# The four merge products of a hybrid encoder block: from channel form to token form

## The chip, the cores and the metric

The kernel runs on one core of a Trainium2 chip. The metric is the device time of one execution in microseconds (us), lower is better. The core has TensorE (PE, matmuls, with a separate row PEld for its weight loads), VectorE (DVE), ScalarE (ACT) and GpSimd (POOL), and queues that start DMAs; the weights come through the queue of SyncE (SP). Each engine works through its own list of instructions in order.

## What is computed

A block with 256 tokens and 2048 channels: a gated linear attention (GLA) branch and a Hyena branch run side by side, are merged by two sigmoid gates, projected, and followed by LayerNorm and an MLP. The part that the change touches is the merge:

```python
y_gla = _gla_branch(q, k, v, r, af, ab, ...)
y_hy = _hyena_branch(hy_u, ...)
g = jax.nn.sigmoid(gate_logits).reshape(B, L, N_BRANCH, D)
merged = g[:, :, 0, :] * (y_gla @ w_gla_o) + g[:, :, 1, :] * (y_hy @ w_hy_o)
mix = merged @ w_out
h = _layernorm(DEEPNORM_ALPHA * h + mix, ln1_g, ln1_b)
```

The gate logits are two more products of the input x, with 2048 columns each. So four products of size 256 x 2048 x 2048 make up the merge. The kernel calls them g1 (first gate), go (GLA output), g2 (second gate) and ho (Hyena output).

## The kernel before

**Products.** Every fp32 operand is split into a high and a low part (`split_hi_lo`, L80): ScalarE casts the high part (L81), VectorE subtracts it from the source for the low part (L82). A product is then high x high + high x low + low x high. Weights come in blocks of 128 x 2048 values, 1 MB each (L95), and each block is split in two halves of 1024 columns (`whi`, `wlo`, three buffers each).

There are two forms of a product:

- **Channel form** (`channel_pair`, L157, with `channel_products`, L136): the result has channels on partitions and tokens along the row. The weights are loaded into TensorE, and the activations move through: for each of 16 slices of the 2048 inputs, one matmul with the high weights moves 512 columns (256 tokens, high and low part side by side, L142), and one with the low weights moves 256 (L146). A block of weights gives 128 channels. ScalarE copies the low half of the PSUM bank out (L154), and VectorE adds the high half to it (L155): `channel_sum`, at high priority.
- **Token form** (`token_group`, L198, with `token_products`, L183): the result has tokens on partitions and 512 channels along the row. The activations are loaded into TensorE, and 512 columns of weights move through: for each slice and each of the two halves of the tokens, three matmuls (L194 to L196). Four blocks of weights give 512 channels, in two PSUM banks, and nothing has to be added afterwards.

Before the change, the products r and v of GLA, the projection w_out (wo) and the second MLP product (w2) are in token form; the rest are in channel form, the four merge products among them.

**Order of the work.** All blocks of weights lie in the order of use in one array `wblk`. Side work (GLA heads, Hyena chunks, filters) is put off by `later(d, fn)` (L110), which runs a function `d` blocks later, when `pump` (L114) is called after a block; `drain` (L122) runs all that is left. A scheduler at build time then sets the order of each engine's list by the order in the program, priorities and its own estimate of when operands are ready; `tc.high_priority()` puts instructions ahead.

**Around the merge.** During the v products and g1 (L632) the side work is GLA's heads: gates (`gla_gates`, L480, with the exponentials and logarithms L504, L505, L517), scores and outputs (`gla_out`, L585). Its last step is a chain over ScalarE (L212, L213) and VectorE (L214 to L217, L599) that ends in the transposes yt on TensorE (L606). The g1 results lie in the buffers `q_sb` and `k_sb`; their sigmoids (L638) stand in the program behind all of this. Then come 8 Hyena chunks of 6 blocks each (uv, ux, uz), with the go products spread among them by `go_after` (L750), in pairs of blocks; each pair is multiplied into the g1 gates (L748). Then g2 with its sigmoids (L773), a drain, and ho, whose results are multiplied by the second gate (L785), added (L786) and split (L787) into `mT`, which has channels on partitions, as w_out needs it. `mT` shares its buffer with the input `xT`. The w_out products follow (L864). Matmuls write to PSUM banks: four for the products (`mmp`), four for the side work (`sdp`).

Of the kernel before, what the change touches and what calls it, by code (L numbers as in the profile page):

```python
# [9 lines left out]
F32 = mybir.dt.float32  # L10
F32R = mybir.dt.float32r
I32 = mybir.dt.int32
AF = mybir.ActivationFunctionType
ALU = mybir.AluOpType
DRAM = bass.MemoryType.DRAM

P = 128
# [23 lines left out]
def block_kernel(  # L41
# [38 lines left out]
    def split_hi_lo(hi, lo, src):  # L80
        nc.scalar.copy(hi, src)  # L81
        nc.vector.tensor_tensor(lo, src, hi.bitcast(F32), op=ALU.subtract)  # L82
# [74 lines left out]
    def channel_pair(act, name, dst=None, scale=1.0):  # L157
        if dst is None:
            dst = base.tile([P, 2, L], F32, tag="sum", name=f"{name}_s")
        for c in range(2):  # L160
            ps = channel_psum(f"{name}_{c}")
            parts = next_block()
            for h in range(2):
                channel_products(ps, act, parts[h], range(8 * h, 8 * h + 8))
            channel_sum(dst[:, c], ps, f"{name}_l{c}", scale)
            pump()
        return dst
# [458 lines left out]

    m_sb = [q_sb, k_sb]

    def m_pair(c2):
        return m_sb[c2 // 4][:, 2 * (c2 % 4):2 * (c2 % 4) + 2, :]  # L630

    for c2 in range(8):  # L632
        channel_pair(xT, f"g1_{c2}", m_pair(c2))
    drain()
    gstk.close()
    for c2 in range(8):
        mp = m_pair(c2)
        nc.scalar.activation(mp, mp, AF.Sigmoid)  # L638


    hstk = ExitStack()
# [98 lines left out]

    go_done = [0]

    def gla_o_pair():
        c2 = go_done[0]
        go_done[0] += 1
        ps = channel_pair(yT, f"go{c2}")
        mp = m_pair(c2)
        nc.vector.tensor_tensor(mp, mp, ps, op=ALU.mult)  # L748

    go_after = [0, 0, 1, 1, 1, 1, 1, 3]  # L750
    for c in range(NCH):
        ps = channel_pair(xT, f"uv{c}")
        cst[("v", c)] = short_conv(ps, 2 * c, f"cv{c}", "cv", 2)
        later(1, hy_v(c))
        later(3, hy_fwd(c, 0))
        later(3, hy_mul(c, 0))
        ps = channel_pair(xT, f"ux{c}")
        cst[("x1c", c)] = short_conv(ps, 16 + 2 * c, f"cx{c}", "cx", 1)
        later(1, hy_x1(c))
        later(5, hy_inv(c, 0))  # L760
        later(6, hy_fwd(c, 1))
        later(6, hy_mul(c, 1))
        ps = channel_pair(xT, f"uz{c}")
        cst[("x2", c)] = short_conv(ps, 32 + 2 * c, f"cz{c}", "cz", 2)
        later(8, hy_inv(c, 1))
        for _ in range(go_after[c]):
            gla_o_pair()


    g2_sb = qp.tile([P, KT, L], F32, tag="G", name="g2_sb")  # L770
    for c2 in range(8):
        ps = channel_pair(xT, f"g2_{c2}")
        nc.scalar.activation(g2_sb[:, 2 * c2:2 * c2 + 2, :], ps, AF.Sigmoid)  # L773
    drain()
    yhT = act_tile(base, "yT", "yh")
    for c in range(NCH):
# [1 line left out]
        nc.gpsimd.dma_start(yr, yh_dram[c])  # L778
        split_hi_lo(yhT[:, 2 * c:2 * c + 2, 0], yhT[:, 2 * c:2 * c + 2, 1], yr)
    mT = act_tile(base, "xT", "mT")  # L780
    for c2 in range(8):
        ps = channel_pair(yhT, f"ho{c2}")
        gp2 = g2_sb[:, 2 * c2:2 * c2 + 2, :]
        mp = m_pair(c2)
        nc.vector.tensor_tensor(gp2, gp2, ps, op=ALU.mult)  # L785
        nc.vector.tensor_tensor(mp, mp, gp2, op=ALU.add)  # L786
        split_hi_lo(mT[:, 2 * c2:2 * c2 + 2, 0], mT[:, 2 * c2:2 * c2 + 2, 1], mp)  # L787
    hstk.close()
    qkg.close()

# [184 lines left out]
def _layout(a):  # L975
    import numpy as np

    f = np.float32

    def chan(w):  # L980
        k, n = w.shape
        return w.reshape(k // P, P, n // P, P).transpose(2, 1, 0, 3).reshape(n // P, P, -1)

    def tok(w):
        k, n = w.shape
        return (w.reshape(k // 512, 4, P, n // 512, 512).transpose(3, 0, 2, 1, 4)
                .reshape(-1, P, D))

    w_in = a["w_in"][0]
    names = ["q", "k", "v", "r", "af", "ab", "u", "g"]  # L990
    sizes = [1024, 1024, 2048, 2048, 16, 16, 6144, 4096]
    seg, s = {}, 0
    for n, z in zip(names, sizes):
        seg[n] = w_in[:, s:s + z]
        s += z
    z16 = np.zeros((D, 32), f)
    ga = np.concatenate([seg["af"], seg["ab"]] * 3 + [z16], axis=1)
    u = chan(seg["u"]).reshape(3, NCH, 2, P, D)
    go = chan(a["w_gla_o"][0])
    ubl, gi = [], 0  # L1000
    for c, n in enumerate([0, 0, 1, 1, 1, 1, 1, 3]):
        for t in range(3):
            ubl.append(u[t, c])
        ubl.append(go[gi:gi + 2 * n])
        gi += 2 * n
    f1 = chan(a["w_ff1"][0])
    w2 = a["w_ff2"][0]
    f1q = [f1[16 * i:16 * (i + 1)] for i in range(QT)]
    f2q = [tok(w2[D * i:D * (i + 1)]) for i in range(QT)]
    g1, g2 = chan(seg["g"][:, :D]), chan(seg["g"][:, D:])  # L1010
    wblk = np.concatenate(
        [chan(ga), chan(seg["q"]), chan(seg["k"]), tok(seg["r"]), tok(seg["v"]), g1]
        + ubl + [g2, chan(a["w_hy_o"][0]), tok(a["w_out"][0])]
        + [f1q[0], f1q[1], f2q[0], f1q[2], f2q[1], f1q[3], f2q[2], f2q[3]], axis=0)

    wa2 = np.zeros((HEADS, P, 512), f)
    for h in range(HEADS):
        cs = slice(h * 256, (h + 1) * 256)
        for r0 in (0, 32, 64):
            wa2[h, r0:r0 + 16, 0:256] = a["gla_wa2_f"][0][:, cs]  # L1020
            wa2[h, r0 + 16:r0 + 32, 256:512] = a["gla_wa2_b"][0][:, cs]
    ba = np.stack([a["gla_ba_f"][0].reshape(8, P).T, a["gla_ba_b"][0].reshape(8, P).T], axis=1)
    cw = a["hy_conv_w"][0].reshape(3, 48, P).transpose(2, 1, 0)
    convp = np.concatenate([cw, a["hy_conv_b"][0].reshape(48, P).T[:, :, None]], axis=2)
    mlp_w = np.zeros((P, 3, P), f)
    for i, n in enumerate(("hy_w1", "hy_w2", "hy_w3")):
        w = a[n][0]
        mlp_w[:w.shape[0], i, :64] = w
        mlp_w[:w.shape[0], i, 64:] = w
    mlp_c = np.stack([np.tile(a[n][0], 2) for n in ("hy_b1", "hy_b2", "hy_b3", "hy_freq")], axis=1)  # L1030
    w4 = a["hy_w4"][0].reshape(64, 2, 2, NCH, CW)
    b4 = a["hy_b4"][0].reshape(2, 2, NCH, CW)
    sk = a["hy_skip"][0].reshape(2, NCH, CW)
    w4s = np.zeros((NCH * 2, P, 2, 512), f)
    for c in range(NCH):
        for o in range(2):
            w = w4[:, o, :, c].reshape(64, 512)
            t = w4s[c * 2 + o]
            t[:64, 0] = w
            t[64:, 0] = w  # L1040
            t[:64, 1] = w
            t[64, 1] = b4[o, :, c].reshape(512)
            t[96, 1] = b4[o, :, c].reshape(512)
            t[65, 1, CW:] = sk[o, c]
            t[97, 1, CW:] = sk[o, c]
    ln_rows = np.concatenate([a["ln1_g"], a["ln1_b"], a["ln2_g"], a["ln2_b"]], axis=0)

    n = np.arange(P)[:, None]
    fr = np.arange(P)[None, :]
    th = 2 * np.pi * (fr + 0.5) * n / 256.0  # L1050
    C, S = np.cos(th), np.sin(th)
    sg = np.where(np.arange(P) % 2 == 0, 1.0, -1.0)
    lo_rows = np.where((np.arange(P) < 64) | (np.arange(P) >= 96), 1.0, 0.0)
    sgn = np.stack([sg, -sg, lo_rows], axis=1).astype(f)
    dft = np.stack([C, -S, C.T / P, -S.T / P], axis=1).astype(f)
    l2c = np.zeros((P, 2, L), f)
    l2c[64, 0, :] = 1.0
    l2c[96, 0, :] = 1.0
    l2c[64, 1, 1:P] = 1.0
    l2c[96, 1, 1:P] = 1.0  # L1060
    l2c[65, 1, 0] = 1.0
    l2c[97, 1, 0] = 1.0
    t = np.linspace(0.0, 1.0, L, dtype=f)[:, None]
    bands = 16
    fb = np.linspace(1e-4, bands - 1, bands, dtype=f)
    wpos = (f(2.0 * math.pi) * np.arange(L, dtype=f) / f(L)).astype(f)
    ang = wpos[:, None] * fb[None, :]
    e = np.concatenate([t, np.cos(ang), -np.sin(ang)], axis=-1)
    emb = np.zeros((P, L), f)
    emb[:33] = e.T  # L1070
    dl = np.abs(np.linspace(math.log(1e-2) / 1.5, math.log(1e-2) / 0.3, D, dtype=f))
    decay = np.exp(-t * dl[None, :]).astype(f)
    up = np.triu(np.ones((64, 64), np.int32))
    mask = np.concatenate([up, 1 - up], axis=0).astype(np.int32)
    sc = np.ones((P, 260), f)
    sc[:, 0::64] = 0.0
    return {
        "x": a["x"][0], "xt": a["x"][0].T.reshape(KT, P, L).transpose(1, 0, 2), "wblk": wblk, "wa2": wa2, "ba": ba, "norm_g": a["gla_norm_g"],
        "convp": convp, "mlp_w": mlp_w, "mlp_c": mlp_c, "emb": emb, "w4s": w4s,
        "ln_rows": ln_rows, "ident_in": np.eye(P, dtype=f), "dft_in": dft,  # L1080
        "sgn_in": sgn, "l2c_in": l2c, "decay_in": decay, "mask_in": mask, "scan_in": sc,
    }
# [17 lines left out]
```

## Time and profile before

| | us |
|---|---|
| median of 3 runs | 1874.85 |
| lowest and highest | 1874.76, 1878.57 |
| the profiled execution's own time | 1875.42 |
| its span, from first to last instruction | 1873.6 |
| g1 products | 358.40 to 469.20 |
| Hyena chunks with the go products | 469.21 to 880.41 |
| g2 products | 880.30 to 970.75 |
| ho products | 970.75 to 1059.82 |

All times inside the profile count from the start of the span. A row of the timeline has the start, the length, the engine, the line of the kernel, the operation, output and inputs with shapes, how many instructions are put together, and in brackets how long the engine stood idle before and for what. A matmul's length is longer than the time that it keeps the next one waiting, since matmuls are pipelined: from the start of one run of matmuls to the start of the next is what they cost. In the rows of groups, three durations with slashes are the smallest, the median and the largest in ns. In the table of stretches, each engine has its busy time and, in brackets, its number of instructions; the last three numbers of a row are the granted TensorE clock (1 is full speed), the busy share of the DMA engines and GB/s.

### The profile page before, as it was taken

How to read it: one execution, taken by the hardware profiler on the slowest of the kernel's cores; microseconds unless marked ns; L12 is line 12 of the kernel's file. 1: busy time of each engine (PE TensorE's matmuls, PEld its weight loads, DVE VectorE, ACT ScalarE, POOL GpSimd, SP SyncE). 2: the span in 40 equal slices, each digit the busy share in tenths (PEclk: the TensorE clock that was granted, in tenths of full speed). 3: DMA queues.
4: the chain of work that ended last, by engine and by line, in shares of the span. 5: the costliest groups of instructions: out<-in, count | busy, mean ns of one | idle time of the engine just before them, and what ended most of it. 6: DMA issues, size and time to landing. Idle time of an engine off the chain costs nothing.

```text
span 1873.6 us, 25223 instructions
## 1 busy us (share of the span) xinstructions
PE 1858.0 (99%) x9948; PEld 1598.3 (85%) x9948; DVE 1307.2 (70%) x1688; ACT 959.0 (51%) x1338; POOL 30.8 (2%) x61
## 2 busy tenths in 40 slices
PE   9999999999999999999999999999999999999998
PEld 7888888888888888888888889888888888888887
DVE  6888878765799999888556668656555655565556
ACT  5555558676555555554544445444434443444332
POOL 1000000000000000000000000000000000000000
PEclk9999999999999999999999999999999999999999
DMA  8677664435555555555555655555555555554553
GB/s 293 210 252 272 246 237 159 155 140 191 195 199 198 199 202 194 197 215 201 208 192 190 256 218 190 191 189 194 183 199 190 193 185 197 190 192 187 195 192 123
DMA packets 60549, 375.06 MB, mean 200 GB/s; under 512 B 6832, under 2 KB 9552, under 8 KB 21008
## 3 DMA queue, kind: packets, MB, share of 16 engines
q1 hardware_dynamic: 47376, 324.03, 46.9%
q0 software_dynamic: 6288, 30.16, 4.4%
q10 hardware_dynamic: 6768, 19.27, 2.9%
q8 instruction: 78, 1.28, 0.3%
q14 instruction: 39, 0.32, 0.0%
HBM read 356.66 MB, written 16.78 MB: 199 GB/s over the span
## 4 chain that ended last, share of the span: by engine, by line
PE 90%; issue 4%; ACT 2%; DMA 2%; DVE 1%; SPq 0%; POOL 0%; DVEq 0%; POOLq 0%; ACTq 0%
PE f L142 12%; PE f L146 7%; PE w L195 6%; PE w L194 6%; PE w L196 6%; PE g L142 4%; PE uv L142 3%; PE ho L142 3%; PE ux L142 3%; PE uz L142 3%; PE g L146 2%; PE go L142 2%; PE ho L146 2%; PE uv L146 2%; PE r L195 2%
## 5 line engine op out<-in xcount | busy, mean ns | idle before, releaser
L82 DVE TENSOR_TENSOR wlo<-raw,whi 128x1024 fp32r<-128x1024 f32 (+2 forms) x603 | 727.7, 1210 | 283.6 <-ACT whi L81 278.8
L81 ACT CAST whi<-raw 128x1024 fp32r<-128x1024 f32 (+2 forms) x603 | 625.7, 1039 | 346.5 <-PE w L196 188.2
L142 PE MATMUL f<-hT,whi 128*128 128x512 f32 (+1 forms) x1048 | 246.7, 386 | 0.0
L142 PEld LDWEIGHTS f<-hT,whi 128*128 128x128 f32 x1048 | 190.0, 188 | 35.5
L195 PE MATMUL w<-wlo,f 128*128 128x512 f32 x480 | 186.7, 389 | 0.0
L196 PE MATMUL w<-whi,f 128*128 128x512 f32 x480 | 186.7, 389 | 0.0
L194 PE MATMUL w<-whi,f 128*128 128x512 f32 x480 | 167.4, 389 | 0.0
L146 PEld LDWEIGHTS f<-hT,wlo 128*128 128x128 f32 x1048 | 134.1, 191 | 4.8
L146 PE MATMUL f<-hT,wlo 128*128 128x256 f32 (+1 forms) x1048 | 135.8, 282 | 0.0
L142 PE MATMUL g<-xT,whi 128*128 128x512 f32 x512 | 125.9, 395 | 0.2 <-ACT whi L81 0.2
L142 PEld LDWEIGHTS g<-xT,whi 128*128 128x128 f32 x512 | 94.5, 190 | 18.7 <-ACT whi L81 0.6
L154 ACT ACTIVATE f_l<-f 128x256 f32<-128x256 f32 x64 | 24.5, 384 | 162.9 <-PE f L142 162.9
L194 PEld LDWEIGHTS w<-whi,f 128*128 128x128 f32 x480 | 90.1, 188 | 18.7
L196 PEld LDWEIGHTS w<-whi,f 128*128 128x128 f32 x480 | 90.1, 188 | 18.7
L195 PEld LDWEIGHTS w<-wlo,f 128*128 128x128 f32 x480 | 90.1, 188 | 18.7
L155 DVE SCALAR_TENSOR_TENSOR f_s<-f,f_l 128x256 f32<-128x256 f32 x64 | 27.2, 424 | 108.5 <-ACT f_l L154 108.5
L146 PEld LDWEIGHTS g<-xT,wlo 128*128 128x128 f32 x512 | 66.1, 191 | 4.5 <-DVE wlo L82 2.1
L146 PE MATMUL g<-xT,wlo 128*128 128x256 f32 x512 | 68.1, 284 | 1.6 <-DVE wlo L82 1.6
L142 PE MATMUL ux<-xT,whi 128*128 128x512 f32 x256 | 64.6, 393 | 0.0
L142 PE MATMUL uz<-xT,whi 128*128 128x512 f32 x256 | 64.5, 393 | 0.0
L142 PE MATMUL go<-yg,whi 128*128 128x512 f32 x256 | 63.6, 392 | 0.0
L142 PE MATMUL uv<-xT,whi 128*128 128x512 f32 x256 | 63.6, 391 | 0.0
(361 smaller groups left out, 3021.0 us busy)
## 6 DMA issues: line engine op xcount, KB each, us to landing
raw<-wblk SPq DMA_DIRECT2D x302, 1024.0 KB, 4.8
Td<-T POOLq DMA_DIRECT2D x16, 768.0 KB, 4.4
Tl<-Td POOLq DMA_DIRECT2D x16, 768.0 KB, 4.6
w<-w4s ACTq DMA_DIRECT2D x16, 512.0 KB, 5.0
zr<-ln_rows ACTq DMA_DIRECT2D x4, 1024.0 KB, 10.8
raw<-wblk SPq DMA_DIRECT2D x11, 256.0 KB, 6.8
dec<-decay_in ACTq DMA_DIRECT2D x8, 256.0 KB, 4.3
yd<-yo POOLq DMA_DIRECT2D x8, 256.0 KB, 4.2
```

Of the source, the lines that this page charges most:

```text
L81: nc.scalar.copy(hi, src)
L82: nc.vector.tensor_tensor(lo, src, hi.bitcast(F32), op=ALU.subtract)
L142: MM(ps[:, :, ts], hi[:, js], act[:, kt, :, ts], start=(kt == 0 and opens), stop=(kt == KT - 1))
L146: MM(ps[:, 0, ts], lo[:, js], act[:, kt, 0, ts], start=False, stop=False)
L154: nc.scalar.activation(low, ps[:, 1], AF.Copy, scale=scale)
L155: nc.vector.scalar_tensor_tensor(dst, ps[:, 0], scale, low, op0=ALU.mult, op1=ALU.add)
L194: MM(pss[tb], sh, wh, start=(kt == 0), stop=False)
L195: MM(pss[tb], sh, wl, start=False, stop=False)
L196: MM(pss[tb], sl, wh, start=False, stop=(kt == KT - 1))
```

## The change

All four merge products take the token form, four groups of 512 columns each. A group of g1 leaves PSUM by one copy on ScalarE and one on VectorE; the sigmoids follow later as before, four instead of eight. A group of go is multiplied into the gate straight from PSUM, and the sigmoid of g2 reads PSUM too. The go groups stand after chunks 1, 3, 5 and 7. After ho, the merged result has tokens on partitions, so 32 transposes of 128 x 128 on TensorE (four groups of eight) turn it, and the split reads it from PSUM. The weights of the four products are laid out for the token form.

```diff
-    for c2 in range(8):
-        channel_pair(xT, f"g1_{c2}", m_pair(c2))
+    def m_group(g):
+        t = m_sb[g // 2][:, 4 * (g % 2):4 * (g % 2) + 4, :]
+        return t.rearrange("p a l -> p (a l)").rearrange("p (t d) -> p t d", t=NT)
+
+    for g in range(4):
+        pss = token_group(xT, f"g1_{g}")
+        mg = m_group(g)
+        with tc.high_priority():
+            nc.scalar.copy(mg[:, 0], pss[0])
+            nc.vector.tensor_copy(mg[:, 1], pss[1])
     drain()
     gstk.close()
-    for c2 in range(8):
-        mp = m_pair(c2)
-        nc.scalar.activation(mp, mp, AF.Sigmoid)
+    for g in range(4):
+        mg = m_group(g)
+        nc.scalar.activation(mg, mg, AF.Sigmoid)
...
-        ps = channel_pair(yT, f"go{c2}")
-        mp = m_pair(c2)
-        nc.vector.tensor_tensor(mp, mp, ps, op=ALU.mult)
-
-    go_after = [0, 0, 1, 1, 1, 1, 1, 3]
+        pss = token_group(yT, f"go{g}")
+        mg = m_group(g)
+        for tb in range(NT):
+            nc.vector.tensor_tensor(mg[:, tb], mg[:, tb], pss[tb], op=ALU.mult)
+
+    go_after = [0, 1, 0, 1, 0, 1, 0, 1]
...
-    g2_sb = qp.tile([P, KT, L], F32, tag="G", name="g2_sb")
-    for c2 in range(8):
-        ps = channel_pair(xT, f"g2_{c2}")
-        nc.scalar.activation(g2_sb[:, 2 * c2:2 * c2 + 2, :], ps, AF.Sigmoid)
+    g2_sb = qp.tile([P, 4, NT, 512], F32, tag="G", name="g2_sb")
+    for g in range(4):
+        pss = token_group(xT, f"g2_{g}")
+        for tb in range(NT):
+            nc.scalar.activation(g2_sb[:, g, tb], pss[tb], AF.Sigmoid)
     drain()
...
-    for c2 in range(8):
-        ps = channel_pair(yhT, f"ho{c2}")
-        gp2 = g2_sb[:, 2 * c2:2 * c2 + 2, :]
-        mp = m_pair(c2)
-        nc.vector.tensor_tensor(gp2, gp2, ps, op=ALU.mult)
-        nc.vector.tensor_tensor(mp, mp, gp2, op=ALU.add)
-        split_hi_lo(mT[:, 2 * c2:2 * c2 + 2, 0], mT[:, 2 * c2:2 * c2 + 2, 1], mp)
+
+    def merged(g):
+        def run():
+            mg = m_group(g)
+            for k2 in range(2):
+                pt = psum_side(f"mt{g}{k2}")
+                for kk in range(2):
+                    for tb in range(NT):
+                        kt = 2 * k2 + kk
+                        nc.tensor.transpose(
+                            pt[:, kk * L + tb * P:kk * L + (tb + 1) * P],
+                            mg[:, tb, kt * P:(kt + 1) * P], ident)
+                s = slice(4 * g + 2 * k2, 4 * g + 2 * k2 + 2)
+                split_hi_lo(mT[:, s, 0], mT[:, s, 1], pt.rearrange("p (a b) -> p a b", a=2))
+        return run
+
+    for g in range(4):
+        pss = token_group(yhT, f"ho{g}")
+        mg = m_group(g)
+        for tb in range(NT):
+            gt = g2_sb[:, g, tb]
+            nc.vector.tensor_tensor(gt, gt, pss[tb], op=ALU.mult)
+            nc.vector.tensor_tensor(mg[:, tb], mg[:, tb], gt, op=ALU.add)
+        later(1, merged(g))
+    drain()
     hstk.close()
...
-    go = chan(a["w_gla_o"][0])
+    go = tok(a["w_gla_o"][0])
...
-    g1, g2 = chan(seg["g"][:, :D]), chan(seg["g"][:, D:])
+    g1, g2 = tok(seg["g"][:, :D]), tok(seg["g"][:, D:])
```

In the layout of `wblk`, the go blocks stand four at a time behind the blocks of chunks 1, 3, 5 and 7, and `w_hy_o` takes the token layout as well.

More of the change, by code (lines that the diff above doesn't have):

```diff
@@ L627, in block_kernel @@
     m_sb = [q_sb, k_sb]
-    def m_pair(c2):
-        return m_sb[c2 // 4][:, 2 * (c2 % 4):2 * (c2 % 4) + 2, :]
-    for c2 in range(8):
-        channel_pair(xT, f"g1_{c2}", m_pair(c2))
+    def m_group(g):
[7 more added lines that the diff above has]
+            nc.vector.tensor_copy(mg[:, 1], pss[1])
     drain()
     gstk.close()
-    for c2 in range(8):
-        mp = m_pair(c2)
-        nc.scalar.activation(mp, mp, AF.Sigmoid)
+    for g in range(4):
+        mg = m_group(g)
+        nc.scalar.activation(mg, mg, AF.Sigmoid)
     hstk = ExitStack()
@@ L741, in block_kernel, with gla_o_group @@
     go_done = [0]
-    def gla_o_pair():
-        c2 = go_done[0]
+    def gla_o_group():
+        g = go_done[0]
         go_done[0] += 1
-        ps = channel_pair(yT, f"go{c2}")
-        mp = m_pair(c2)
-        nc.vector.tensor_tensor(mp, mp, ps, op=ALU.mult)
-    go_after = [0, 0, 1, 1, 1, 1, 1, 3]
+        pss = token_group(yT, f"go{g}")
[3 more added lines that the diff above has]
+    go_after = [0, 1, 0, 1, 0, 1, 0, 1]
     for c in range(NCH):
@@ L766, in block_kernel @@
         for _ in range(go_after[c]):
-            gla_o_pair()
-    g2_sb = qp.tile([P, KT, L], F32, tag="G", name="g2_sb")
-    for c2 in range(8):
-        ps = channel_pair(xT, f"g2_{c2}")
-        nc.scalar.activation(g2_sb[:, 2 * c2:2 * c2 + 2, :], ps, AF.Sigmoid)
+            gla_o_group()
+    g2_sb = qp.tile([P, 4, NT, 512], F32, tag="G", name="g2_sb")
[3 more added lines that the diff above has]
+            nc.scalar.activation(g2_sb[:, g, tb], pss[tb], AF.Sigmoid)
     drain()
@@ L998, in _layout @@
     u = chan(seg["u"]).reshape(3, NCH, 2, P, D)
-    go = chan(a["w_gla_o"][0])
+    go = tok(a["w_gla_o"][0])
     ubl, gi = [], 0
-    for c, n in enumerate([0, 0, 1, 1, 1, 1, 1, 3]):
+    for c, n in enumerate([0, 1, 0, 1, 0, 1, 0, 1]):
         for t in range(3):
             ubl.append(u[t, c])
-        ubl.append(go[gi:gi + 2 * n])
-        gi += 2 * n
+        ubl.append(go[gi:gi + 4 * n])
+        gi += 4 * n
     f1 = chan(a["w_ff1"][0])
@@ L1009, in _layout @@
     f2q = [tok(w2[D * i:D * (i + 1)]) for i in range(QT)]
-    g1, g2 = chan(seg["g"][:, :D]), chan(seg["g"][:, D:])
+    g1, g2 = tok(seg["g"][:, :D]), tok(seg["g"][:, D:])
     wblk = np.concatenate(
         [chan(ga), chan(seg["q"]), chan(seg["k"]), tok(seg["r"]), tok(seg["v"]), g1]
-        + ubl + [g2, chan(a["w_hy_o"][0]), tok(a["w_out"][0])]
+        + ubl + [g2, tok(a["w_hy_o"][0]), tok(a["w_out"][0])]
         + [f1q[0], f1q[1], f2q[0], f1q[2], f2q[1], f1q[3], f2q[2], f2q[3]], axis=0)
```

## The prediction

> **What bounds the kernel now.** I read the page first, then the table of waits of TensorE, then the table of stretches, and last the timeline around the four products. The page:
>
> ```profile
> span 1873.6 us, 25223 instructions
> PE 1858.0 (99%) x9948; PEld 1598.3 (85%) x9948; DVE 1307.2 (70%) x1688; ACT 959.0 (51%) x1338; POOL 30.8 (2%) x61
> PE 90%; issue 4%; ACT 2%; DMA 2%; DVE 1%; SPq 0%; POOL 0%; DVEq 0%; POOLq 0%; ACTq 0%
> ```
>
> TensorE is busy for 99% of the span and holds 90% of the chain that ended last. So what counts is how long TensorE needs for its list of matmuls, and the few places where it waits. The longest of those, of all waits of TensorE (what waited, for what: us in total, times, longest):
>
> ```profile
> PE ht L887 <- DVE zr L837: 2.0, 2, 1.4
> PE yt L606 <- DVE rq_t L216: 2.0, 1, 2.0
> PE g L146 <- DVE wlo L82: 1.6, 2, 1.0
> ```
>
> The table of stretches (length, then busy us of TensorE, its weight loads, VectorE, ScalarE and GpSimd, then the granted clock) shows the v products, the g1 products, one Hyena chunk with two go blocks, the ho products, and three groups of w_out:
>
> ```profile
> 253.00:358.40 105.40, 105.40 (x521) 87.95 (x520) 82.16 (x143) 80.37 (x167) 1.06 (x2) 1.00 0.50 183
> 358.40:469.20 110.80, 107.78 (x645) 93.98 (x644) 68.24 (x113) 74.77 (x128) 0.53 (x1) 0.98 0.44 163
> 594.86:647.54 52.68, 52.68 (x299) 46.10 (x298) 48.34 (x58) 29.14 (x41) 1.60 (x3) 1.00 0.54 195
> 970.75:1059.82 89.07, 89.07 (x513) 78.72 (x512) 58.01 (x69) 42.86 (x56) 0.00 (x0) 1.00 0.53 190
> 1059.82:1125.10 65.28, 65.28 (x289) 54.05 (x288) 38.94 (x43) 30.06 (x30) 0.00 (x0) 1.00 0.70 264
> ```
>
> TensorE has no gap in v, in the chunk, in ho and in w_out. In g1 it is idle for 3.0 us and its clock is 0.98.
>
> **The four products: -8.1 us.** g1, go, g2 and ho are 16 blocks of weights each, 64 in all. The channel form takes 32 matmuls a block (16 with 512 moving columns, 16 with 256); the token form takes 24, all with 512. The columns are the same, 12288 a block, so only what an instruction costs beyond its columns can be saved. TensorE in ho, one block:
>
> ```profile
> 974.48 3.82 PE L142 MATMUL ho<-yh,whi 128*128 128x512 f32 x16
> 978.13 2.08 PE L146 MATMUL ho<-yh,wlo 128*128 128x256 f32 x16
> 980.05 3.82 PE L142 MATMUL ho<-yh,whi 128*128 128x512 f32 x16
> ```
>
> From start to start, 16 wide ones take 978.13 - 974.48 = 3.65 us (228 ns each) and 16 narrow ones 1.92 us (120 ns). 256 more columns thus cost 108 ns, and 228 - 2 x 108 leaves some 11 ns that an instruction costs whatever its width. The stretches say it without a model: ho is 89.07 / 16 = 5.567 us a block, w_out in token form 65.28 / 12 = 5.440. The difference, 0.127 us, times 64 is **8.1 us**. The other bound comes from the 11 ns alone: 8 instructions fewer x 11 ns x 64 = 5.8 us. I take 8.1, since w_out is the form itself. The v stretch is token form amid the side work of the gated linear attention (GLA), and it has no gap, so I expect the form to hold in g1 and go too.
>
> [...]
>
> **The transposes: +3.0 us.** Four groups of 8, so 32, new on TensorE. The rows nearest are those of yt, yT and ht, each 128 x 128 with the same identity; of each, one run and what TensorE started next:
>
> ```profile
> 403.58 0.82 PE L606 MATMUL yt<-ident,y 128*128 128x128 f32 x6
> 404.15 0.48 PE L146 MATMUL g<-xT,wlo 128*128 128x256 f32 x2
> 894.72 0.60 PE L733 MATMUL yT<-ident,zg 128*128 128x128 f32 x4
> 895.08 0.36 PE L146 MATMUL g<-xT,wlo 128*128 128x256 f32 x1
> 1148.35 1.25 PE L887 MATMUL ht<-ident,zr 128*128 128x128 f32 x10
> 1149.36 0.72 PE L142 MATMUL f<-hT,whi 128*128 128x256 f32 x4
> ```
>
> 0.57 / 6, 0.36 / 4 and 1.01 / 10 are 95, 90 and 101 ns each; 32 x 95 = **3.0 us** (2.9 to 3.2). If each held TensorE for its whole duration, it would be far more:
>
> ```profile
> L606 PE MATMUL yt<-ident,y x32: 270/272/445, 334.2 to 437.3; 128*128 128x128 f32 x32
> L733 PE MATMUL yT<-ident,zg x32: 270/272/273, 557.5 to 895.0; 128*128 128x128 f32 x32
> ```
>
> 32 x 0.272 = 8.7 us, which would eat the 8.1; but the starts show that they overlap.
>
> [...]
>
> **The wait ahead of the transposes: +1.0 us.** A group's transposes need two multiplies and two adds on VectorE first, 2 x 0.691 + 2 x 0.685 = 2.8 us by the rows of today's forms:
>
> ```profile
> L785 DVE TENSOR_TENSOR g_sb<-g_sb,ho_s x8: 691/691/692, 983.0 to 1060.9; 128x512 f32<-128x512 f32 x8
> L786 DVE TENSOR_TENSOR q_sb<-q_sb,g_sb x4: 685/685/685, 984.7 to 1018.1; 128x512 f32<-128x512 f32 x4
> ```
>
> For groups 0 to 2 the code puts the transposes one block (5.4 us) later, so a block of products hides the 2.8 us. The last group comes in the drain. What hides it is w_out's first group, which reads the last four slices of mT only in its fourth block, 16.3 us on. That needs the scheduler to put those products ahead of the transposes in TensorE's queue, which is in order: what is queued behind a waiting transpose is w_out itself. The price without cover is 2.8 us plus ScalarE's share. Neighbours: 32 yT transposes wait for nothing, 32 yt and 32 ht wait 2.2 and 2.0 us. I take the middle, 1.0, with ends 0 and 2.8.
>
> **Work off TensorE: 0.** The 64 channel sums go (0.38 us on ScalarE, 0.42 on VectorE each); 4 copies on each engine come for g1; multiplies, adds, sigmoids and splits keep their sizes, some now reading PSUM. Both engines get some 20 us lighter, hidden behind TensorE before and after. The g2 sigmoids and the go multiplies now free the PSUM banks, but there are four banks, and a group uses two for some 22 us. Weight DMAs keep number, size and queue.
>
> **Where go stands among the Hyena chunks: +1.2 us.** A chunk has 6 blocks of its own. Before, two go blocks follow each of chunks 2 to 6; after, four follow chunks 1, 3, 5, 7, so chunks 2, 4, 6 have none. Take the chunk at 594.86 and remove its go pair:
>
> ```profile
> L82 DVE TENSOR_TENSOR wlo<-raw,whi 128x1024 fp32r<-128x1024 f32 (+2 forms) x603 | 727.7, 1210 | 283.6 <-ACT whi L81 278.8
> L155 DVE SCALAR_TENSOR_TENSOR go_s<-go,go_l x16: 415/419/425, 595.4 to 881.0; 128x256 f32<-128x256 f32 x16
> L748 DVE TENSOR_TENSOR q_sb<-q_sb,go_s x4: 683/685/686, 602.1 to 755.3; 128x512 f32<-128x512 f32 x4
> ```
>
> VectorE: 48.34 - 4 x 1.21 - 2 x 0.42 - 0.69 = 41.9 us. TensorE: 52.68 - 2 x 5.57 = 41.5. VectorE goes from 92% of the chunk to 101%. A chunk with four go blocks comes to 53.0 of 63.3 us, 84%, so the excess of 0.4 us can be worked off there. If it can't, three chunks cost 3 x 0.4 = **1.2 us**, which I take. Lower end 0; upper end in the rivals.
>
> **The stall in g1: -3.3 us.** ScalarE, then TensorE:
>
> ```profile
> 378.63 1.28 ACT L638 ACT_TABLE_LOAD   x1
> 381.51 1.28 ACT L504 ACT_TABLE_LOAD   x1
> 385.18 1.28 ACT L505 ACT_TABLE_LOAD   x1
> 390.30 1.28 ACT L213 ACT_TABLE_LOAD   x1
> 386.78 3.82 PE L142 MATMUL g<-xT,whi 128*128 128x512 f32 x16
> 393.24 2.00 PE L142 MATMUL g<-xT,whi 128*128 128x512 f32 x8
> 397.20 0.66 PE L606 MATMUL yt<-ident,y 128*128 128x128 f32 x2 [1.96 <-DVE rq_t L216]
> 398.09 3.29 PE L142 MATMUL g<-xT,whi 128*128 128x512 f32 x8 [0.23 <-ACT whi L81]
> 401.22 1.00 PE L573 MATMUL s<-qi,kk 128*128 128x64 f32 x8
> ```
>
> A sigmoid of g1's first pair slips in at 378.63, ahead of the exponentials and logarithms of GLA's last head. Four table loads of 1.28 us follow within 13 us; the chain to yt comes late, TensorE waits 1.96 us, and the next 8 products take 401.22 - 398.09 = 3.13 us instead of 1.82, the half clock behind the 0.98. Together 1.96 + 1.31 = 3.3 us. After the change the first sigmoid needs a whole group of four blocks. The first 8 of the 16 products at 386.78 end today's fourth block, at some 388.6 us; this sigmoid can't come before, and by then that head's exponentials, no longer held up by the load at 378.63, are well under way. I take it that this stall goes: **-3.3**. Nothing is late in its place by the nearest row, the v stretch: three heads of the same work, no sigmoid, no gap. Ends: all that g1 loses today, 3.0 idle + 1.7 clock = -4.7; or the same again, as the later sigmoid lands between another head's steps, +3.3.
>
> **The sum.** -8.1 + 3.0 + 1.0 + 1.2 - 3.3 = -6.2 us. The profiled execution took 1875.42 us (its span 1873.6 and 1.8 around it), so 1869.2 on its scale. It lies 0.57 above the median of the three runs, 1874.85; on that scale **1868.6 us**.
>
> **Rivals.**
> 1. The g1 stall stays or moves: -2.9, 1872.0 us. For it: sigmoids still mix with GLA's exponentials, since the scheduler puts them wherever ScalarE is free. Against: the date above. Chance 0.23.
> 2. VectorE binds in chunks 2, 4 and 6. For it: 101%. Against: at 92% there was no gap, and the next chunk has room. It decides when the low halves of weights come so late that TensorE stands for 2 us, as in g1, and drops to half clock: 3.3 us in each of three chunks, 9.9. With the g1 stall staying, -8.1 + 3.0 + 1.0 + 9.9 = +5.8, 1880.6 us: slower. Chance 0.18.
> 3. The matmuls cost their columns alone, so nothing is saved, or the transposes cost 8.7: with the other terms and the stall, +5.2 or +2.8, 1880.1 or 1877.6 us. Against: ho and w_out. Chance 0.06. [...]
>
> That the change does not do what it says is ruled in or out by the counts: 64 x 8 = 512 matmuls fewer, 32 more.
>
> **How the numbers follow.** The forecast has 0.53, the rivals 0.23, 0.18 and 0.06. The low end is -8.1 + 2.9 - 4.7 and the 1.0 us wait for wlo in the products g: -10.9, 1864.0. The high end, 1877.0, takes in rival 1 and the mild part of rivals 2 and 3. A measurement of this kernel tells about 0.2% (3.7 us) from no change. Faster by more 0.53, within 0.25, slower by more 0.22.
>
> **What would show it.** TensorE's records fall from 9948 to about 9468. The ho stretch shrinks from 89.07 to some 87.0 plus 2.3 for three groups of transposes. The mt transposes show 90 to 100 ns from start to start, and little wait. In g1 no half clock and no wait of yt for rq_t. In the stretches of chunks 2, 4, 6 VectorE is near 100%, TensorE without gaps. It is wrong if token blocks take over 5.5 us, if TensorE waits for wlo in the chunks, or if a new wait of 2 us brings the half clock.

## The result and the profile after

| | before | after |
|---|---|---|
| median of 6 runs each, us | 1875.62 | 1869.19 |
| lowest and highest | 1873.10, 1878.57 | 1867.45, 1869.99 |
| the profiled execution's own time | 1875.42 | 1867.45 |

The ratio is 0.996, with a 95% interval of 0.995 to 0.997: faster by 0.3 to 0.5%. In a second set of runs (e8 below) the same two kernels gave 1867.39 and 1877.06, ratio 0.9948 (0.9935 to 0.9962), so the gain is 6.4 us by the medians of the first set and 9.7 by those of the second. The median of the kernel before alone lies between 1875.62 and 1877.62 in the four sets in which it ran. The forecast was 1868.6.

The page of the changed kernel:

```profile
span 1865.7 us, 24010 instructions
PE 1853.5 (99%) x9468; PEld 1575.7 (84%) x9468; DVE 1285.6 (69%) x1628; ACT 937.7 (50%) x1270; POOL 30.9 (2%) x61
PE 97%; DVE 1%; DMA 1%; ACT 1%; issue 0%; SPq 0%; DVEq 0%; ACTq 0%
```

TensorE has 9468 matmuls, as the count of the change says (9948 - 512 + 32). Its busy time falls by 4.5 us, the span by 7.9. The rest shows in its waits:

```profile
PE ht L912 <- DVE zr L862: 2.0, 2, 1.4
PE yt L606 <- DVE rs L217: 0.8, 1, 0.8
```

The wait of ht in the LayerNorm is the same as before. The 2.0 us of yt for rq_t and the 1.6 us of g for wlo are gone; 0.8 us of yt are left, at another place. Now the stretches (length, busy us of TensorE, its weight loads, VectorE, ScalarE, GpSimd, granted clock): g1; Hyena with go and g2; ho; w_out; the first half of the MLP. After:

```profile
358.75:463.34 104.59, 103.76 (x517) 86.21 (x516) 63.88 (x101) 66.84 (x109) 0.54 (x1) 1.00 0.47 172
463.34:959.70 496.36, 496.36 (x2593) 425.54 (x2592) 404.37 (x465) 262.80 (x353) 16.69 (x31) 1.00 0.55 202
959.70:1049.43 89.73, 89.73 (x409) 74.58 (x408) 49.95 (x51) 37.45 (x40) 0.00 (x0) 1.00 0.51 188
1049.43:1139.86 90.43, 90.43 (x501) 79.15 (x500) 59.00 (x80) 41.20 (x46) 0.00 (x0) 1.00 0.63 244
1139.86:1327.40 187.54, 185.45 (x1095) 164.94 (x1094) 118.96 (x152) 90.00 (x124) 0.00 (x0) 0.99 0.50 186
```

Before, the same stretches where the prediction has not shown them:

```profile
469.21:970.75 501.54, 500.52 (x2849) 438.99 (x2848) 414.74 (x496) 271.08 (x384) 16.61 (x31) 1.00 0.54 200
1059.82:1149.36 89.54, 89.54 (x494) 78.31 (x492) 57.97 (x78) 40.95 (x46) 0.00 (x0) 1.00 0.65 246
1149.36:1335.35 185.99, 183.91 (x1096) 163.39 (x1094) 118.85 (x152) 89.85 (x124) 0.00 (x0) 1.00 0.51 188
```

| stretch | before | after | difference |
|---|---|---|---|
| up to g1 | 358.40 | 358.75 | +0.35 |
| g1 | 110.81 | 104.59 | -6.22 |
| Hyena, go, g2 | 501.54 | 496.36 | -5.18 |
| ho (24 of the transposes in it) | 89.07 | 89.73 | +0.66 |
| w_out (8 transposes in it) | 89.54 | 90.43 | +0.89 |
| first half of the MLP | 185.99 | 187.54 | +1.55 |
| the rest | 538.26 | 538.27 | +0.01 |

The sum is -7.94 us, the difference of the spans. The last difference of any size, +1.55, lies where the change edits nothing. Its cause is a spell of half clock in the profiled execution of after (0.51 granted from 1150.0 to 1151.8 us), which the one of before has in g1 (0.59 from 398.09 to 401.22 us) and not there (more on this at the end).

### The profile page after: what moved, and what is told of

Its sections match the earlier page's. It is cut to its first block, busy times and chain, and to the rows that moved or that the text cites. A ratio compares the mean times of both kernels' runs of the same rounds, so it can differ in the third digit from the quotient of the medians.

```text
span 1865.7 us, 24010 instructions
## 1 busy us (share of the span) xinstructions
PE 1853.5 (99%) x9468; PEld 1575.7 (84%) x9468; DVE 1285.6 (69%) x1628; ACT 937.7 (50%) x1270; POOL 30.9 (2%) x61
## 4 chain that ended last, share of the span: by engine, by line
PE 97%; DVE 1%; DMA 1%; ACT 1%; issue 0%; SPq 0%; DVEq 0%; ACTq 0%
PE f L142 12%; PE f L146 7%; PE w L196 6%; PE w L195 6%; PE w L194 6%; PE ux L142 3%; PE uz L142 3%; PE uv L142 3%; PE g L196 3%; PE g L195 3%; PE g L194 3%; PE ux L146 2%; PE uv L146 2%; PE uz L146 2%; PE r L195 2%; PE k L142 2%
## 5 line engine op out<-in xcount | busy, mean ns | idle before, releaser
L195 PE MATMUL g<-wlo,xT 128*128 128x512 f32 x256 | 100.0, 391 | 0.0
L196 PE MATMUL g<-whi,xT 128*128 128x512 f32 x256 | 99.7, 390 | 0.0
L194 PE MATMUL g<-whi,xT 128*128 128x512 f32 x256 | 92.3, 390 | 0.0
L194 PEld LDWEIGHTS g<-whi,xT 128*128 128x128 f32 x256 | 48.1, 188 | 9.9
L195 PEld LDWEIGHTS g<-wlo,xT 128*128 128x128 f32 x256 | 48.1, 188 | 9.9
```

Source lines behind the costliest of these rows:

```text
L194: MM(pss[tb], sh, wh, start=(kt == 0), stop=False)
L195: MM(pss[tb], sh, wl, start=False, stop=False)
L196: MM(pss[tb], sl, wh, start=False, stop=(kt == KT - 1))
```

## The experiments

**Theory.** The gain has two sources: the token form saves 2.0 us a product, and the g1 stall goes because the first sigmoid, and with it the table loads on ScalarE, comes later. The 32 transposes take some 3 us of it back. **Rivals:** the stall went because the token form leaves ScalarE and VectorE more time, or by chance; the transposes cost their full duration, or nothing; VectorE binds in the chunks without go. The kernel before was run again beside each experiment, the changed kernel only in the first set and in e8. Times that were expected by counting from its first median, 1869.2, therefore carry the 1.8 us between these two sets, and where less than that is at stake the stretches decide.

### The sigmoids held back, nothing else changed (e1)

```diff
-        nc.scalar.activation(mp, mp, AF.Sigmoid)
+        tc.keep_in_program_order(nc.scalar.activation(mp, mp, AF.Sigmoid))
```

> The kernel before (1875.6 us), all products in channel form, with one edit: the eight sigmoids of g1 are pinned behind the last step of g1 on ScalarE, so that none falls between the exponentials and logarithms of GLA. Theory (the stall in g1 comes from the table loads that the early sigmoid brings, and goes when the sigmoid comes later): the 1.96 us wait of yt for rq_t and the half clock behind it go, some 4 us in all; 1871 to 1872 us, g1 stretch 105 to 107 us instead of 110.8. Rival (the stall went because the token form leaves ScalarE and VectorE more time, and the place of the sigmoid has nothing to do with it): no change, g1 stretch 110 to 111.

Measured: 1873.66 against 1876.69 us, ratio 0.9987 (0.9979 to 0.9996), a smaller gain than expected. Of ScalarE's timeline in and behind g1, the only table load that is left, and of the stretches, g1:

```profile
470.88 1.28 ACT L638 ACT_TABLE_LOAD   x1
```

```profile
363.32:469.35 106.03, 106.03 (x646) 93.24 (x645) 68.22 (x113) 58.52 (x111) 0.54 (x1) 1.00 0.48 170
```

All matmuls are in channel form as before, and VectorE has the same 68.2 us of work, but TensorE has no gap, the clock is 1.00, and g1 takes 106.03 instead of 110.81 us: -4.8. ScalarE has 16 us less to do here, sigmoids and table loads. The stall hangs on the place of the sigmoids, and the rival falls: the token form is not needed for it. In the medians only 3.0 of the 4.8 us arrive (0.8 to 3.9 by the interval). Some 1.3 us of the 4.8 is half clock (in before, 3.13 us for eight products whose share of 16 is 1.82), which does not come with the stall each time (e5).

### The same in the changed kernel (e2)

```diff
-        nc.scalar.activation(mg, mg, AF.Sigmoid)
+        tc.keep_in_program_order(nc.scalar.activation(mg, mg, AF.Sigmoid))
```

> The changed kernel (1869.2 us) with the four sigmoids of g1 pinned behind the last step of g1 on ScalarE. Theory: the one gap that is left in g1, 1.0 us ahead of yt at 430 us, goes with the four table loads between 423 and 430 us; 1868.2 us, g1 stretch 103.6 instead of 104.6. Rival (that gap is the chain of GLA's last head itself, whatever the tables): 1869.2. A second risk: the sigmoids now stand in one piece ahead of the first Hyena chunk and hold up ScalarE's casts of weights there; then TensorE shows gaps after 463 us.

Measured: 1869.11 us, ratio to before 0.9952 (0.9939 to 0.9965). The stretches of g1 and of Hyena with go and g2:

```profile
357.99:461.49 103.50, 103.50 (x518) 86.36 (x517) 64.19 (x101) 56.37 (x100) 0.54 (x1) 1.00 0.49 174
461.49:958.13 496.64, 496.64 (x2593) 425.55 (x2592) 404.26 (x465) 266.94 (x357) 16.69 (x31) 1.00 0.57 202
```

g1 falls by 1.1 us, where 1.0 was expected, and no gap comes behind it, though the stretch behind it is 0.3 us longer. In the medians, 1.1 us drowns. With e1 this also gives g1 free of stalls in both forms: 106.03 and 103.50, a difference of 2.5 us where the form alone was priced at 2.0.

### No transposes (e3)

```diff
-                pt = psum_side(f"mt{g}{k2}")
...
-                        nc.tensor.transpose(
-                            pt[:, kk * L + tb * P:kk * L + (tb + 1) * P],
-                            mg[:, tb, kt * P:(kt + 1) * P], ident)
...
-                split_hi_lo(mT[:, s, 0], mT[:, s, 1], pt.rearrange("p (a b) -> p a b", a=2))
+                split_hi_lo(mT[:, s, 0], mT[:, s, 1], mg[:, k2].rearrange("p (a b) -> p a b", a=2))
```

> The changed kernel without the 32 transposes: the merged result, still with tokens on partitions, is split straight from SBUF into mT, so this kernel leaves the turn of the merged result out. Theory (a transpose costs TensorE 95 to 100 ns in the stream and nothing waits): 3.1 us less than the changed kernel, 1866.1. Rival (a transpose costs its 272 ns duration, or the wait ahead of it): 8.7 us less, 1860.5. Other rival (they fill gaps that TensorE has anyway): no difference.

Measured: 1864.86 us, ratio to before 0.9934 (0.9921 to 0.9948). The stretches of ho and w_out:

```profile
960.66:1047.70 87.04, 87.04 (x385) 72.10 (x384) 49.70 (x51) 38.03 (x40) 0.00 (x0) 1.00 0.54 193
1047.70:1137.24 89.54, 89.54 (x493) 78.33 (x492) 58.94 (x80) 41.22 (x46) 0.00 (x0) 1.00 0.66 247
```

Against after, ho loses 89.73 - 87.04 = 2.69 us and w_out 90.43 - 89.54 = 0.89, together 3.58: 112 ns a transpose. Both rivals fall. The 87.04 is also the clean token form of ho, 2.03 us under the 89.07 of the channel form.

### g1 alone in token form (e4)

The edit takes over the new `m_group` and the g1 loops of the change, and their weight layout, into the kernel before.

> The kernel before with g1 alone in token form (its gates then lie in token order and are multiplied with the channel form of go, so the pairing of elements in the merge is left wrong). Theory: 2.0 us for 16 blocks of 5.44 instead of 5.57 us, and some 4 us for the stall, about -6: 1869.6 us, g1 stretch 104.6. Rival (the stall is a matter of chance in each schedule, and only the matmul form counts): -2.0, 1873.6, g1 stretch 108 or more.

Measured: 1870.42 against 1876.69 us, ratio 0.9965 (0.9951 to 0.9978). Its g1, and its Hyena with go and g2:

```profile
362.17:466.77 104.60, 103.77 (x517) 86.18 (x516) 63.88 (x101) 66.83 (x109) 0.54 (x1) 1.00 0.47 172
466.77:967.04 500.27, 500.27 (x2850) 439.04 (x2849) 415.25 (x496) 271.57 (x384) 16.68 (x31) 1.00 0.56 201
```

104.60 as in the changed kernel: one product of the four, and 6 us of gain, because most of the stall goes with it. The second row has go and g2 in channel form, and no gap for wlo in g2, though nothing was edited there.

### g1 alone back in channel form (e5)

The mirror image: the changed kernel with the g1 loops and the g1 weight layout of before.

> The changed kernel with g1 put back into channel form, its eight sigmoids placed as before (the gates lie in channel order while the rest of the merge is in token order, so the pairing of elements is left wrong). Theory: the 2.0 us of the g1 products and the stall of some 4 us come back, so about +6 against the changed kernel, 1875.2, no faster than the kernel before: three products' 6 us and the wait of 1.2 us in g2 are balanced by 3.1 us of transposes, 1871.5, plus whatever the stall costs in this schedule. Rival (the stall is not bound to g1's form): 1871.2, only the 2.0 us of products come back.

Measured: 1873.56 against 1877.62 us, ratio 0.9981 (0.9972 to 0.999); no gain over the kernel before was expected. Of ScalarE's timeline up to 396 us the table loads, of TensorE's the stall, and the stretch of g1:

```profile
381.67 1.28 ACT L642 ACT_TABLE_LOAD   x1
384.55 1.28 ACT L504 ACT_TABLE_LOAD   x1
388.22 1.28 ACT L505 ACT_TABLE_LOAD   x1
393.33 1.28 ACT L213 ACT_TABLE_LOAD   x1
```

```profile
400.23 0.44 PE L606 MATMUL yt<-ident,y 128*128 128x128 f32 x2 [1.96 <-DVE rq_t L216]
401.12 2.12 PE L142 MATMUL g<-xT,whi 128*128 128x512 f32 x8 [0.45 <-ACT whi L81]
403.08 1.00 PE L573 MATMUL s<-qi,kk 128*128 128x64 f32 x8
```

```profile
361.44:471.07 109.63, 106.38 (x645) 93.00 (x644) 68.26 (x113) 74.64 (x128) 0.53 (x1) 1.00 0.47 164
```

The four loads are back and so is the wait of 1.96 us, to the hundredth. But here the 8 products behind it take 1.96 us (403.08 - 401.12), where before they took 3.13: the same wait, and no half clock (the stretch has 1.00, that of before 0.98). So g1 gives back 5.0 of its 6.2 us (109.63 - 104.59).

### All go groups behind the last chunk (e6)

```diff
-    go_after = [0, 1, 0, 1, 0, 1, 0, 1]
+    go_after = [0, 0, 0, 0, 0, 0, 0, 4]
```

The blocks in `wblk` are put in the same order.

> The changed kernel with all four go groups behind the last Hyena chunk, so that eight chunks of 6 blocks follow each other and VectorE is asked for 101% of each from the third on. Theory from the result (the scheduler lets Hyena's steps slip behind the weights, so the excess does not reach TensorE; the slipped steps are done in the go blocks at the end): no gap, the time of the changed kernel, 1869.2 within 0.5 us. Rival (VectorE binds once there is no 10-block chunk to recover in): at least 0.4 us in each of six chunks, 2.4 us, and some 3.3 us for each stall of 2 us that brings the half clock: 1871.6 to 1880.

Measured: 1868.10 us, ratio to before 0.9945 (0.9931 to 0.9958). Hyena with go and g2, a piece of 40 us of the chunks that now follow each other, and the go blocks behind them:

```profile
464.30:960.69 496.39, 496.39 (x2593) 425.81 (x2592) 404.36 (x465) 262.65 (x353) 16.64 (x31) 1.00 0.57 202
585.00:625.00 40.00, 40.00 (x228) 35.04 (x228) 37.67 (x48) 22.06 (x33) 1.08 (x2) 1.00 0.61 211
774.16:873.16 99.00, 99.00 (x445) 81.92 (x444) 80.13 (x79) 45.47 (x52) 3.24 (x6) 1.00 0.57 201
```

496.39 against 496.36 us: the place of go costs nothing. VectorE is at 94% in the piece shown, and at 90 to 95% in pieces of 39 or 40 us from 546 to 742 us, not at 101%. Four of the 16 multiply steps of Hyena (`hy_mul`, by their last addition, L712) end behind 774 us, beside go; by the counts in `later` one of them is due there.

### g2 alone in token form (e7)

```diff
-    for c2 in range(8):
-        ps = channel_pair(xT, f"g2_{c2}")
-        nc.scalar.activation(g2_sb[:, 2 * c2:2 * c2 + 2, :], ps, AF.Sigmoid)
+    for g in range(4):
+        pss = token_group(xT, f"g2_{g}")
+        gv = g2_sb[:, 4 * g:4 * g + 4, :].rearrange("p a l -> p (a l)").rearrange("p (t d) -> p t d", t=NT)
+        for tb in range(NT):
+            nc.scalar.activation(gv[:, tb], pss[tb], AF.Sigmoid)
```

The g2 weights take the token layout as well.

> The kernel before with g2 alone in token form (its gates lie in token order and are multiplied with the channel form of ho, so the pairing of elements is left wrong). g2 has no GLA beside it. Theory: 16 blocks x 0.127 us = 2.0 us, and the 1.0 us wait for wlo at 911 us may go: -2.0 to -3.2, 1872.4 to 1873.6, g2 stretch 87 us of products instead of 89.3. Rival (matmuls cost their columns alone and the gain sits elsewhere): no change, or -1.0 for the wait.

Measured: 1874.76 against 1877.62 us, ratio 0.9987 (0.9978 to 0.9996). Hyena, go and g2:

```profile
470.26:968.51 498.25, 498.25 (x2721) 432.32 (x2720) 408.90 (x481) 267.42 (x369) 16.61 (x31) 1.00 0.57 201
```

Before, this stretch was 501.54 with 500.52 busy. The 3.3 us fall apart into 500.52 - 498.25 = 2.3 of products and 1.0 of the gap for wlo.

### The changed kernel again, and the two free edits together (e8, e9)

> The changed kernel once more, unaltered, so that the next kernel is compared with it on the same chip. By the stretches of the traces so far (products 8.1 us less, transposes 3.6 more, g1's stall 4.2 less, g2's wait 1.2 less) it should lie some 8 to 10 us under the kernel before where both have the half clock the same number of times, and 6 to 8 by the medians, since the half clock comes and goes at the transposes ht: ratio 0.995 to 0.997.

Measured: 1867.39 against 1877.06 us, ratio 0.9948 (0.9935 to 0.9962), with the stretches of the first trace of the changed kernel: 104.60 in g1, 496.36 in Hyena, go and g2.

> The changed kernel with both edits that cost nothing so far: the g1 sigmoids pinned behind g1, and all four go groups behind the last Hyena chunk. Theory (the remaining gap of 1 us in g1 goes, the place of go is indifferent): 1.1 us under the changed kernel, g1 stretch 103.5 us, Hyena with g2 496.4 us as in the changed kernel. Rival (the held sigmoids and the denser chunks meet on ScalarE and VectorE in the first chunks): Hyena with g2 over 497.5 us, nothing gained.

Measured on the same chip: 1866.90 us, ratio to before 0.9947 (0.9935 to 0.996).

```profile
358.83:462.32 103.49, 103.49 (x518) 86.36 (x516) 64.16 (x101) 56.35 (x100) 0.53 (x1) 1.00 0.49 173
462.32:959.00 496.68, 496.68 (x2593) 425.80 (x2592) 404.13 (x465) 266.79 (x357) 16.64 (x31) 1.00 0.57 202
```

Against the changed kernel the stretches gain 1.1 us in g1 and give 0.3 back behind it. The medians of e8 and e9 differ by 0.5 us, which these runs can't tell from nothing.

## Why the prediction was right, term by term

| term | predicted | measured | by |
|---|---|---|---|
| four products | -8.1 | -8.2 to -8.7 | ho 2.03 (e3), go and g2 4.16, g1 2.5 (e1 against e2) or 2.0 (priced like ho) |
| transposes | +3.0 | +3.6 | e3 |
| wait ahead of them | +1.0 | 0 | after |
| place of go | +1.2 | 0 | e6 |
| stall in g1 | -3.3 | -3.7 to -4.2 | g1's 6.22 less the product |
| wait for wlo in g2 | 0 | -1.0 | stretches; not tied to the edit |
| half clock elsewhere, start | 0 | +1.55, +0.35 | stretches; not tied to the edit |

The total of -6.2 stands against -6.4 and -9.7 in the medians of the two sets and -7.9 between the two profiled executions. The first five rows are what the change accounts for: they sum to -6.2 as predicted and to about -8.8 as measured. The last two rows differ between the two executions, and no run ties them to the edit. So the way and the main causes were right, and the size was forecast too small: two costs of 2.2 us together did not come. That the forecast lies only 0.6 us below the first median of the changed kernel is in part luck.

**The products** were right in cause and size, since the price came from whole stretches of both forms: after, TensorE is busy for 500.52 - 496.36 = 4.16 us less in the stretch with go and g2. The 11 ns that the prediction worked out for an instruction would give only 5.8 us. Its rows show where most of the rest lies: two narrow matmuls take 2 x 120 = 240 ns and one wide one in token form 5.440 / 24 = 0.2267 us, so each of the 512 saves an estimated 13.3 ns, 6.8 us in all. The wide ones, 228 ns in the channel form, bring the other 1.3 us; why they differ, no run isolates.

**The transposes** were priced from their own starts, 95 ns. In the changed kernel, TensorE's timeline around the first eight:

```profile
987.36 1.03 PE L797 MATMUL mt<-ident,q_sb 128*128 128x128 f32 x8
988.15 0.48 PE L195 MATMUL ho<-wlo,yh 128*128 128x512 f32 x1
988.46 0.39 PE L196 MATMUL ho<-whi,yh 128*128 128x512 f32 x1
```

0.79 us for eight is 99 ns each, within the 90 to 100 of the forecast. But the first product behind them takes 988.46 - 988.15 = 0.31 us instead of 0.227. Such a switch was left out of the sum; 3.58 us counts it in.

**The wait ahead of them** did not come, as the cover that the prediction named held: the transposes come after the multiplies and adds are done, also the last eight, which the scheduler put 5.9 us behind the start of w_out (w_out's first products and the last transposes, in the same timeline):

```profile
1049.43 0.61 PE L194 MATMUL wo<-whi,mT 128*128 128x512 f32 x2
...
1055.33 1.03 PE L797 MATMUL mt<-ident,k_sb 128*128 128x128 f32 x8
```

**The place of go** is where a step failed. The sum for VectorE, 41.9 us of work in a chunk of 41.5, took it that a chunk must do its own side work. Chunks 2 and 3 of after, the first without go and the second with it:

```profile
561.39:601.43 40.04, 40.04 (x229) 35.02 (x227) 33.03 (x42) 21.84 (x31) 1.08 (x2) 1.00 0.53 194
601.43:663.69 62.26, 62.26 (x327) 53.37 (x325) 56.74 (x66) 33.49 (x45) 2.14 (x4) 1.00 0.55 205
```

VectorE is at 82% where the forecast had 101, and at 91% where it had 84. TensorE too needs 40.0 us instead of 41.5. Hyena's steps move into the blocks of go: of its multiply steps (L706 to L712) one ends in chunk 2 and three end in chunk 3. In part this is the program's order, since `later` puts a chunk's second multiply ten blocks behind its start, so a chunk of 6 blocks hands it on. That the steps can fall behind further, e6 shows. Rival 2 rested on the same step.

**The stall in g1** went for the reason given. ScalarE in the changed kernel, from head 3's exponentials to the first sigmoid:

```profile
378.34 0.68 ACT L504 ACTIVATE ga<-ga 128x512 f32<-128x512 f32 x1
...
388.88 1.54 ACT L523 ACTIVATE e<-gb 128x64 f32<-128x64 f32 x6
...
393.10 1.28 ACT L643 ACT_TABLE_LOAD   x1
```

The first table load comes at 393.10, behind that head's last exponential, where before four had come between 378 and 392. Those four take 5.1 us, the sigmoid among them 0.63. e1 takes the stall away without the token form, e5 brings it back within the changed kernel.

But sigmoids still mix with GLA's steps, as rival 1 held. A second group of loads, in the chain that ends in yt, stands between 428 and 435 us before and is still there after:

```profile
423.19 1.28 ACT L212 ACT_TABLE_LOAD   x1
425.38 1.28 ACT L213 ACT_TABLE_LOAD   x1
426.89 1.28 ACT L212 ACT_TABLE_LOAD   x1
428.50 1.28 ACT L213 ACT_TABLE_LOAD   x1
```

The wait of yt behind it grows from 0.2 to 0.8 us, and e2, which removes these loads too, takes 1.1 us out of g1. So the stall is not wholly gone: of the 4.8 us that e1 takes out, the change gets 4.8 - 1.1 = 3.7. The forecast still left 0.4 to 0.9 us too much standing: the wait for wlo within g1 (0.6 us) and the other delays of the same loads went too.

**The wait for wlo in g2** stood only in the low end of the range. It is absent in e7 with the token form, but in e1 and e4 too, where g2 has the channel form and nothing was edited there. So no run shows that the form takes it away; what brings it, no run here isolates.

## What to carry to other kernels

Where TensorE is busy for 99% and two forms of a product have the same columns, count instructions: here 512 fewer were worth 8 us, some 16 ns each, of which 32 transposes took 3.6 us back. Take the price from whole stretches of both forms: the slope between two widths gave only 11 ns. Look for what the edit does to the order of another engine: another 4 us came from one sigmoid that no longer fell among one head's exponentials. When side work may slip, a window's work is no demand that the window has to meet: here 101% was counted for VectorE in a chunk, and it was busy for 82% of it.

## What was not expected of the hardware

The same wait on TensorE has the half clock behind it in one trace (0.51 granted) and not in another (1.00). At the transposes ht of the LayerNorm every kernel here has the same two waits. After, and then before:

```profile
1148.41 0.63 PE L912 MATMUL ht<-ident,zr 128*128 128x128 f32 x4 [1.40 <-DVE zr L862]
1149.61 0.70 PE L912 MATMUL ht<-ident,zr 128*128 128x128 f32 x4 [0.58 <-DVE zr L862]
1150.00 2.03 PE L142 MATMUL f<-hT,whi 128*128 128x256 f32 x8
1151.82 1.05 PE L912 MATMUL ht<-ident,zr 128*128 128x128 f32 x4
```

```profile
1157.90 0.63 PE L887 MATMUL ht<-ident,zr 128*128 128x128 f32 x4 [1.39 <-DVE zr L837]
1159.10 0.63 PE L887 MATMUL ht<-ident,zr 128*128 128x128 f32 x4 [0.57 <-DVE zr L837]
1159.48 1.20 PE L142 MATMUL f<-hT,whi 128*128 128x256 f32 x8
1160.53 0.60 PE L887 MATMUL ht<-ident,zr 128*128 128x128 f32 x4
```

The eight products behind the waits take 1.82 us in one and 1.05 in the other; the granted clock between 1150.0 and 1151.8 us of after is 0.51, that of before between 1159.4 and 1160.6 is 1.00. It costs some 1.5 us each time: the first half of the MLP takes 187.4 to 187.6 us in seven of the eleven traces (after, e1, e3, e4, e6, e7, e8) and 186.0 in four (before, e2, e5, e9). At the stall in g1 it came in two of three traces: the clock of the g1 stretch is 0.98 in before and in e7 and 1.00 in e5, and the eight products take 3.13 us in before and 1.96 in e5. So the half clock stood behind one wait of 2.0 us and behind two of 1.4 and 0.6 us in a row, and behind the same waits it also stayed away. What decides it no run here shows. For the reader of times it means that two profiled executions can differ by 1.5 us a stall where the code is the same, more than some of the terms above. The start differs by more: the stretch up to g1, in which no run here edits anything, takes 358.0 to 363.3 us in the eleven traces. In e1 it takes 4.9 us more than in before, so its span is 1.6 us longer in spite of the 4.8 us that g1 loses; why, no run here isolates.
